# Eight inner tiles begun early and finished among whole ones, own buffers for the accumulated block, norms in single steps, squares on VectorE

## The chip, the cores and the metric

The kernel runs on one core of one Trainium2 chip. The metric is the device time of one execution, in microseconds (us); less is better. TensorE does the matmuls, VectorE (DVE) and ScalarE (ACT) the element-wise work, GpSimd (POOL) some element-wise work and the issue of transfers that add to their target, SyncE (SP) the issue of most other transfers.

## The reference

One layer of a decoder: 512 prompt tokens and 8 sample tokens of width 2048. The part that the change touches is the end of the first sub-layer and the first half of the second:

```python
x = x + gt1[:, None, :] * (jnp.concatenate([att, rw], axis=-1) @ w_out[l])
h2 = _modulate(_rmsnorm(x, g_norm_ffn[l]), sh2, sc2)
gate, up = jnp.split(h2 @ w_ffn_in[l], 2, axis=-1)     # 2048 -> 2 x 5632
x = x + gt2[:, None, :] * ((jax.nn.silu(gate) * up) @ w_ffn_out[l])
```

where

```python
def _rmsnorm(x, g):
    y = xf * lax.rsqrt(jnp.mean(xf * xf, axis=-1, keepdims=True) + RMS_EPS)
    return (y * g.astype(jnp.float32)).astype(x.dtype)
def _modulate(h, shift, scale):
    return h * (1.0 + scale[:, None, :]) + shift[:, None, :]
```

All is float32. Ahead of it stand the modulation vectors, a first norm, the combined input projection, sliding-window attention and an RWKV-7 mixer; behind it a final norm.

## The kernel before

Features lie on the 128 partitions, tokens along the rows. The 520 tokens are two halves of 260 columns (HB: 256 of the prompt, 4 samples); x is kept as eight tiles `x1[kp]` of two feature blocks each. Float32 precision is had from pairs: a block `t` is cut into `wh` (ScalarE's cast, L1244) and `wl = t - wh` (VectorE, L1245), and each product of 128 x 128 weights with 260 columns is three matmuls: `wh` with the high part, `wh` with the low part, `wl` with the high part of the operand. Four such products, on one loaded block of 128 x 512 weights, are 12 matmuls.

**Out projection, last quarter (`wout_half`).** It is done for half 0, then for half 1: 16 output blocks of 12 matmuls each per half, two to a PSUM tile. After each pair `accumulate_half` adds the gated result to x (VectorE: L1192 for the 256 prompt columns of each block, L1194 and L1195 for the samples), copies the sample columns and stores x (GpSimd, L1197, L1198), squares x (ScalarE, L1200), and adds the squares up in `acc` (GpSimd, L1203 and L1210). `norm` sums them over the partitions by a matmul with ones (L1215), takes the root and VectorE's reciprocal (L1218).

**Norms.** `norm_first` is half 0's norm. It runs as a generator in the background of half 1's matmuls: `pump`, called after each product, takes it one `yield` further. Its result is `B0`, the high and low parts of half 0's operand. `norm_second` is half 1's norm together with the combinations of the two halves that the inner projection needs: B22, T1, T2, T3, T4. It is a generator of 37 steps that `ffn_in` calls by hand. In a pair (`norm_pair`) VectorE multiplies, GpSimd copies the sample columns (L1237), ScalarE scales and shifts (L1239).

**Inner projection (`ffn_in`).** The 5632 pairs of gate and up are 44 inner tiles. In each, the weight rows of gate and up and the two halves of the 2048 features make 2 x 2 blocks a11, a12, a21, a22, and the two halves of tokens the other side; seven products in place of eight give the four results. Each of the seven is 2 groups (g) of 12 matmuls, so a whole tile has 168 matmuls. p1 and p2 (a11 with B11, a12 with B21) need half 0 alone; the other five need half 1's norm. So the first six tiles are *early* ones: their p1 and p2 (48 matmuls) are done while half 1's norm is made, 22 of its 37 steps among them, and their sum goes to DRAM (`pcd`). Then the loop over all 44 tiles runs: tiles 0 to 5 are *old*, take their sum back (`pc`) and do the other five products (120 matmuls); tiles 6 to 43 are whole. The other steps of the norm are taken in tile 0, three after each product.

Per group SyncE loads a11, a21, a12 (tag `sr`, six buffers together), a22 (tag `raw`, three) and s3 (tag `ar`, three). GpSimd issues an accumulating transfer that adds a block of weights to a21 (L1448) and one that adds to s3 (L1451; not in the second group of an old tile). VectorE then adds a21 into a11 (L1457) and a11 into a12 (L1464). When a tile is done, VectorE multiplies (L1412) and GpSimd stores the result `gd` (L1414). The order of the instructions on each engine, and of the issues on each queue, is set by the tile framework's scheduler from the order of the code; each engine takes its instructions in that order.

Of the kernel before, what the change touches and what calls it, by code (L numbers as in the profile page):

```python
# [14 lines left out]
P = 128  # L15
# [48 lines left out]
class Kern:  # L64
    def __init__(self, tc, I, O, upto="all"):
        self.tc, self.nc, self.I, self.O, self.upto = tc, tc.nc, I, O, upto
        self.n = 0
        self.bg = []
        self.free, self.done_at = {}, 0.0
        self.px = PacedCore(self)  # L70
        self.nada = 0
        self.sample_done = self.kv_done = self.decode_done = False
        self.cat_out, self.cat_in = set(), 0
        self.psc = None
        self.squares = [None, None]

# [72 lines left out]
    def run(self):  # L149
        tc, nc, I = self.tc, self.nc, self.I  # L150
        R = dict(side="right")
        with ExitStack() as st:
# [8 lines left out]
            self.x1d = [self.dr.tile([P, 2, 2, HB], F32, name=f"x1d{i}") for i in range(8)]  # L161
            self.pcd = [self.dr.tile([P, 2, HB], F32, name=f"pcd{i}") for i in range(6)]
            self.gd = [self.dr.tile([P, 2, HB], F32, name=f"gd{i}") for i in range(FT)]
# [1022 lines left out]
    def accumulate_half(self, o, n, ps, gt, h):  # L1186
# [12 lines left out]
        sq = self.fp.tile([P, 2, HB], F32, tag="n", bufs=self.nb, name=self.nm("sqh"))[:, 0:n]  # L1199
        nc.scalar.activation(sq, x, AF.Square)  # L1200
        if o == 0:
            acc = self.fp.tile([P, HB], F32, tag=f"acc{h}", name=self.nm("acc"))
            nc.gpsimd.tensor_tensor(acc, sq[:, 0], sq[:, 1], ALU.add)  # L1203
            self.squares[h] = [acc]
        elif n == 1:
            self.squares[h].append(sq[:, 0])
        else:
            acc = self.squares[h][0]
            for j in range(n):
                nc.gpsimd.tensor_tensor(acc, acc, sq[:, j], ALU.add)  # L1210

    def norm(self, h, ps, nc):

        for i, a in enumerate(self.squares[h]):
            nc.tensor.matmul(ps[:, 0:HB], self.ones, a, start=i == 0, stop=i == 2)  # L1215
        r = self.fp.tile([P, HB], F32, tag=f"rstd{h}", name=self.nm("rstdh"))
        nc.scalar.activation(r, ps[:, 0:HB], AF.Sqrt, bias=self.eps_r, scale=1.0 / 2048)
        nc.vector.reciprocal(r, r)  # L1218
        return r
# [11 lines left out]
    def norm_pair(self, nc, h, kp, r, us):  # L1231

        k = 2 * kp
        hb = self.fp.tile([P, 2, HB], F32, tag="n", bufs=self.nb, name=self.nm("hb"))
        nc.vector.tensor_tensor(hb[:, :, 0:256], self.x1[kp][:, :, h, 0:256],
                                r[:, 0:256].unsqueeze(1).broadcast_to([P, 2, 256]), ALU.mult)
        nc.gpsimd.tensor_copy(hb[:, :, 256:HB], us[:, k:k + 2])  # L1237
        for i in range(2):
            nc.scalar.activation(hb[:, i, 0:256], hb[:, i, 0:256], AF.Identity, bias=self.mod[:, SH2 + k + i, 0:1],  # L1239
                                 scale=self.G[:, k + i, 0:1])  # L1240
        return hb

# [4 lines left out]
    def norm_first(self, psum):  # L1247

        nc = self.px
        r = self.norm(0, psum("ssq2"), nc)  # L1250
        yield
        us = self.norm_start(nc, 0, r)
        self.hb0 = []
        for kp in range(8):
            hb = self.norm_pair(nc, 0, kp, r, us)
            self.hb0.append(hb)
            ks = slice(2 * kp, 2 * kp + 2)
            self.cut(nc, self.B0[0][:, ks], self.B0[1][:, ks], hb)
            for _ in range(4):
                self.done_at = self.now()  # L1260
                yield

    def norm_second(self, psum):
# [6 lines left out]
        for kp in range(4):  # L1270
# [7 lines left out]
            yield  # L1278
            less(b12, b22, b12)
            put(self.B22, kp, b22)  # L1280
            yield
            less(b22, b22, b11)
            put(self.T1, kp, b11)
            yield
# [84 lines left out]
    def ffn_in(self, st):  # L1369
# [15 lines left out]
        src = lambda ht, row, col, g: I["w_fi"][2 * ht + row][:, 1024 * col + 512 * g:1024 * col + 512 * g + 512]  # L1385

        def load(ht, row, col, g, tag="sr"):
            pool, n = (self.w, 3) if tag == "raw" else (sp, 6)
            t = pool.tile([P, 512], F32, tag=tag, bufs=n, name=self.nm(tag))
            nc.sync.dma_start(t, src(ht, row, col, g))  # L1390
            return t
# [42 lines left out]
        rest = iter(())  # L1434
        for ht in range(FT):
            pc = ct("pc", 3)
# [6 lines left out]
            for g in range(2):  # L1443
                a11, a21 = load(ht, 0, 0, g), load(ht, 1, 0, g)
                a22 = load(ht, 1, 1, g, "raw")
# [3 lines left out]
                if not (old and g):  # L1449
                    nc.sync.dma_start(s3, src(ht, 0, 0, g))  # L1450
                    nc.gpsimd.dma_start(s3, src(ht, 1, 0, g), accum_op=ALU.add)  # L1451
                if not old:
                    product(p12[:, 0], weights(a11), B11, g)
                    product(p12[:, 1], weights(a12), B21, g)
                    if g == 1:
                        first_sums(pc, p12)
                nc.vector.tensor_tensor(a11, a21, a11, ALU.add)  # L1457
                for ps, a, b in ((p45[:, 1], a21, T1), (p67[:, 0], a11, T2), (p67[:, 1], s3, T3),
                                 (p45[:, 0], a22, T4), (p3[:, 0], a12, B22)):
                    product(ps, weights(a), b, g)  # L1460
                    if b is T1:
# [3 lines left out]
                        next(rest, None)  # L1465
                    if ht == 0:
                        for _ in range(3):
                            next(norm, None)
                    if g == 0:
# [227 lines left out]
```

## Time and profile before

| | |
|---|---|
| three runs | 2688.58, 2691.93 (median), 2697.04 us |
| the profiled execution's own time | 2691.33 us |
| its span | 2689.6 us |
| mean granted TensorE clock | 0.973 |
| TensorE busy | 2576.4 us, 96% of the span |
| VectorE busy | 1707.8 us, 63% |
| ScalarE busy | 1109.5 us, 41% |
| GpSimd busy | 421.8 us, 16% |
| mean DMA rate | 170 GB/s |

The span is the time from the first to the last instruction of the profiled execution; 1.7 us of its own time lie outside it. The granted clock is the share of full speed that TensorE was given. Shares are means over stages of different kinds: the out projection's half 1 begins at 1183.4 us of the span, the early tiles at 1219.8, the old tiles at 1264.9, the whole ones at 1389.4, and they end at 2163.5.

### The profile page before, as it was taken

How to read it: one execution, taken by the hardware profiler on the slowest of the kernel's cores; microseconds unless marked ns; L12 is line 12 of the kernel's file. 1: busy time of each engine (PE TensorE's matmuls, PEld its weight loads, DVE VectorE, ACT ScalarE, POOL GpSimd, SP SyncE). 2: the span in 40 equal slices, each digit the busy share in tenths (PEclk: the TensorE clock that was granted, in tenths of full speed). 3: DMA queues.
4: the chain of work that ended last, by engine and by line, in shares of the span. 5: the costliest groups of instructions: out<-in, count | busy, mean ns of one | idle time of the engine just before them, and what ended most of it. 6: DMA issues, size and time to landing. Idle time of an engine off the chain costs nothing. (4 is left out here: it accounts for less than half of the span.)

```text
span 2689.6 us, 59198 instructions
## 1 busy us (share of the span) xinstructions
PE 2576.4 (96%) x23405; PEld 2366.7 (88%) x23405; DVE 1707.8 (63%) x3825; ACT 1109.5 (41%) x2136; POOL 421.8 (16%) x567
## 2 busy tenths in 40 slices
PE   6899999999999999988889999999999999999997
PEld 4577778787787899887789999999999999999997
DVE  3466676776767355678667777777777763443456
ACT  3133444455533334555334444444444432222225
POOL 1012122122112000043111221212212100000004
PEclk9899899999989999999889999999999999999999
DMA  7965454555556663246677777777777663343333
GB/s 278 324 196 167 123 153 150 159 155 162 152 159 213 206 221 107 92 149 193 181 187 198 194 194 192 196 196 191 199 195 193 165 204 93 122 127 97 120 103 108
DMA packets 241879, 458.10 MB, mean 170 GB/s; under 512 B 33936, under 2 KB 45120, under 8 KB 241568
## 3 DMA queue, kind: packets, MB, share of 16 engines
q1 hardware_dynamic: 206928, 377.78, 43.3%
q0 software_dynamic: 34032, 75.49, 13.5%
q8 instruction: 183, 3.00, 0.5%
q10 hardware_dynamic: 640, 1.05, 0.2%
q14 instruction: 96, 0.79, 0.1%
HBM read 420.15 MB, written 35.06 MB: 169 GB/s over the span
## 5 line engine op out<-in xcount | busy, mean ns | idle before, releaser
L88 ACT CAST wh<-raw 128x512 fp32r<-128x512 f32 (+2 forms) x405 | 246.3, 611 | 489.0 <-PE pf L98 286.6
L98 PE MATMUL pf<-go,wh 128*128 128x260 f32 x2560 | 414.1, 281 | 0.0
L1244 ACT CAST wh<-sr 128x512 fp32r<-128x512 f32 x416 | 258.3, 621 | 367.2 <-PE pm L1404 326.3
L91 DVE TENSOR_TENSOR wl<-raw,wh 128x512 fp32r<-128x512 f32 (+2 forms) x405 | 281.8, 697 | 172.2 <-ACT wh L88 159.2
L98 PEld LDWEIGHTS pf<-go,wh 128*128 128x128 f32 x2560 | 353.9, 188 | 0.1
L1245 DVE TENSOR_TENSOR wl<-sr,wh 128x512 fp32r<-128x512 f32 x416 | 286.8, 690 | 98.4 <-ACT wh L1244 88.8
L98 PE MATMUL pm<-hH,wh 128*128 128x260 f32 (+1 forms) x1248 | 297.5, 318 | 1.7 <-ACT hH L143 1.6
L1404 PE MATMUL pm<-xT,wh 128*128 128x260 f32 x1408 | 269.6, 291 | 1.7 <-ACT wh L1244 1.7
L98 PE MATMUL pf<-go,wl 128*128 128x260 f32 x1280 | 267.7, 282 | 0.0
L98 PE MATMUL pm<-hL,wh 128*128 128x260 f32 (+1 forms) x1248 | 265.0, 292 | 0.2 <-DVE hL L144 0.2
L98 PE MATMUL pm<-hH,wl 128*128 128x260 f32 (+1 forms) x1248 | 262.3, 290 | 0.1
L1404 PE MATMUL pm<-T,wh 128*128 128x260 f32 x1408 | 258.9, 284 | 2.4 <-ACT wh L1244 2.4
L98 PEld LDWEIGHTS pm<-hH,wh 128*128 128x128 f32 (+1 forms) x1248 | 195.5, 192 | 50.2 <-issue 32.3
L1404 PEld LDWEIGHTS pm<-xT,wh 128*128 128x128 f32 x1408 | 223.4, 194 | 7.6 <-ACT wh L1244 2.2
L1404 PEld LDWEIGHTS pm<-T,wh 128*128 128x128 f32 x1408 | 217.6, 189 | 2.8 <-ACT wh L1244 2.8
L1404 PE MATMUL pm<-xT,wl 128*128 128x260 f32 x704 | 196.8, 290 | 16.8 <-DVE wl L1245 16.8
L1404 PE MATMUL pm<-B0H,wl 128*128 128x260 f32 x704 | 199.4, 283 | 5.3 <-DVE wl L1245 5.1
L1404 PE MATMUL pm<-B0H,wh 128*128 128x260 f32 x704 | 200.2, 284 | 3.6 <-DVE acct L1194 2.7
L98 PEld LDWEIGHTS pm<-hH,wl 128*128 128x128 f32 (+1 forms) x1248 | 197.5, 192 | 6.0 <-DVE wl L91 2.1
L98 PEld LDWEIGHTS pm<-hL,wh 128*128 128x128 f32 (+1 forms) x1248 | 198.0, 192 | 5.4 <-issue 2.0
L1404 PE MATMUL pm<-T,wl 128*128 128x260 f32 x704 | 199.2, 284 | 2.0 <-DVE wl L1245 2.0
L98 PEld LDWEIGHTS pf<-go,wl 128*128 128x128 f32 x1280 | 201.0, 188 | 0.0
(417 smaller groups left out, 5196.5 us busy)
## 6 DMA issues: line engine op xcount, KB each, us to landing
sr<-in_w_fi SPq DMA_DIRECT2D x264, 256.0 KB, 3.6
ar<-in_w_ada SPq DMA_DIRECT2D x256, 256.0 KB, 3.1
raw<-in_w_fo SPq DMA_DIRECT2D x176, 256.0 KB, 2.6
raw<-in_w_in SPq DMA_DIRECT2D x148, 256.0 KB, 3.6
araw<-in_w_ada SPq DMA_DIRECT2D x64, 512.0 KB, 6.3
raw<-in_w_fi SPq DMA_DIRECT2D x112, 256.0 KB, 3.3
sr<-in_w_fi POOLq DMA_DIRECT2D x88, 256.0 KB, 4.7
s<-in_w_fi SPq DMA_DIRECT2D x82, 256.0 KB, 3.6
```

Of the source, the lines that this page charges most:

```text
L88: nc.scalar.copy(wh[:, :n], raw[:, :n])
L91: nc.vector.tensor_tensor(wl[:, :n], raw[:, :n], wh[:, :n].bitcast(F32), ALU.subtract)
L98: nc.tensor.matmul(ps[:m, bank, :HB], w, a[:, k, h, :], start=first and i == 0, stop=last and i == 2, skip_group_check=True,)
L1244: nc.scalar.copy(H, src)
L1245: nc.vector.tensor_tensor(L, src, H.bitcast(F32), ALU.subtract)
L1404: nc.tensor.matmul(ps[:, :HB], x[:, s], y, start=g == k == i == 0, stop=g == 1 and k == 3 and i == 2, skip_group_check=True)
```

## The change

1. Eight tiles are early in place of six. The old tiles are no longer the first of the loop: each stands behind four whole ones (places 4, 9, ..., 39).
2. a21 leaves the `sr` buffers. It goes by turns to four buffers of the pool `xp` that hold nothing at that time (tags sq, rstd, sq, acc); a11 and a12 keep the six of `sr`.
3. `norm_first` begins eight steps later and takes six steps for a pair, three ahead of the cut and three behind it, in place of four. `norm_second` has 45 steps with one operation (or one cut) in each; 30 of them are taken in the early tiles, 14 in the first group of the first whole tile, the last ahead of its second group. ScalarE copies the sample columns in place of GpSimd.
4. In the out projection VectorE adds the squares up, those of one accumulation when the next one is made. In the last block, after the second projection, GpSimd goes on doing it at once.

```diff
-            self.pcd = [self.dr.tile([P, 2, HB], F32, name=f"pcd{i}") for i in range(6)]
+            self.pcd = [self.dr.tile([P, 2, HB], F32, name=f"pcd{i}") for i in range(8)]
...
         nc.scalar.activation(sq, x, AF.Square)
+        if gt == GT1:
+            self.add_squares(nc.vector)
+            self.pending = h, o, n, sq
+        else:
+            self.pending = h, o, n, sq
+            self.add_squares(nc.gpsimd)
+
+    def add_squares(self, eng):
+        if not self.pending:
+            return
+        h, o, n, sq = self.pending
+        self.pending = None
         if o == 0:
             acc = self.fp.tile([P, HB], F32, tag=f"acc{h}", name=self.nm("acc"))
-            nc.gpsimd.tensor_tensor(acc, sq[:, 0], sq[:, 1], ALU.add)
+            eng.tensor_tensor(acc, sq[:, 0], sq[:, 1], ALU.add)
             self.squares[h] = [acc]
         elif n == 1:
             self.squares[h].append(sq[:, 0])
         else:
             acc = self.squares[h][0]
             for j in range(n):
-                nc.gpsimd.tensor_tensor(acc, acc, sq[:, j], ALU.add)
+                eng.tensor_tensor(acc, acc, sq[:, j], ALU.add)
 
     def norm(self, h, ps, nc):
 
+        self.add_squares(self.nc.vector)
         for i, a in enumerate(self.squares[h]):
...
-        nc.gpsimd.tensor_copy(hb[:, :, 256:HB], us[:, k:k + 2])
         for i in range(2):
             nc.scalar.activation(hb[:, i, 0:256], hb[:, i, 0:256], AF.Identity, bias=self.mod[:, SH2 + k + i, 0:1],
                                  scale=self.G[:, k + i, 0:1])
+        nc.scalar.copy(hb[:, :, 256:HB], us[:, k:k + 2])
         return hb
...
         nc = self.px
+        def rest(n):
+            for _ in range(n):
+                self.done_at = self.now()
+                yield
+
+        yield from rest(8)
         r = self.norm(0, psum("ssq2"), nc)
         yield
         us = self.norm_start(nc, 0, r)
         self.hb0 = []
         for kp in range(8):
-            hb = self.norm_pair(nc, 0, kp, r, us)
-            self.hb0.append(hb)
+            self.hb0.append(self.norm_pair(nc, 0, kp, r, us))
+            yield from rest(3)
             ks = slice(2 * kp, 2 * kp + 2)
-            self.cut(nc, self.B0[0][:, ks], self.B0[1][:, ks], hb)
-            for _ in range(4):
-                self.done_at = self.now()
-                yield
+            self.cut(nc, self.B0[0][:, ks], self.B0[1][:, ks], self.hb0[kp])
+            yield from rest(3)
...
             less(b12, b22, b12)
+            yield
             put(self.B22, kp, b22)
             yield
             less(b22, b22, b11)
+            yield
             put(self.T1, kp, b11)
...
+        places = (("sq", 2), ("rstd", 1), ("sq", 2), ("acc", 1))
+
         def load(ht, row, col, g, tag="sr"):
             pool, n = (self.w, 3) if tag == "raw" else (sp, 6)
+            if tag in places:
+                pool, (tag, n) = self.xp, tag
             t = pool.tile([P, 512], F32, tag=tag, bufs=n, name=self.nm(tag))
...
-        for ht in range(FT):
+        order = list(range(early, FT))
+        for ht in range(early):
+            order.insert(4 + 5 * ht, ht)
+        for i, ht in enumerate(order):
...
-                a11, a21 = load(ht, 0, 0, g), load(ht, 1, 0, g)
+                a11, a21 = load(ht, 0, 0, g), load(ht, 1, 0, g, places[(2 * i + g) % 4])
...
+                if i == 0 and g == 1:
+                    for _ in norm:
+                        pass
                 if not old:
-                    product(p12[:, 0], weights(a11), B11, g)
-                    product(p12[:, 1], weights(a12), B21, g)
+                    for col, a, b in ((0, a11, B11), (1, a12, B21)):
+                        product(p12[:, col], weights(a), b, g)
+                        if i == g == 0:
+                            next(norm, None)
+                            next(norm, None)
...
-                    if ht == 0:
-                        for _ in range(3):
-                            next(norm, None)
+                    if i == g == 0:
+                        next(norm, None)
+                        next(norm, None)
```

**GpSimd's queue among the old tiles.** Before, from the old tiles on; sr_... is an a21, s_... an s3, gd_130 and gd_131 the results of tiles 0 and 1:

```order
L1448 DMA sr_15861<-in_w_fi 128x512
L1451 DMA s_2222_15867<-in_w_fi 128x512
L1448 DMA sr_15957<-in_w_fi 128x512
L1414 DMA gd_130<-cu_15815 128x520
L1448 DMA sr_16063<-in_w_fi 128x512
L1451 DMA s_2257_16069<-in_w_fi 128x512
L1448 DMA sr_16159<-in_w_fi 128x512
L1414 DMA gd_131<-cu_16017 128x520
```

Now, around the first old tile, at place 4; sq_16891 and rstd_16987 are its a21 of both groups, s_2391_16897 its s3, sq_17093 and acc_17221 the a21 of the whole tile at place 5, and gd_142 and gd_143 the results of the whole tiles at places 2 and 3:

```order
L1474 DMA sq_16891<-in_w_fi 128x512
L1477 DMA s_2367_16756<-in_w_fi 128x512
L1474 DMA rstd_16987<-in_w_fi 128x512
L1477 DMA s_2391_16897<-in_w_fi 128x512
L1437 DMA gd_142<-cu_16576 128x520
L1474 DMA sq_17093<-in_w_fi 128x512
L1474 DMA acc_17221<-in_w_fi 128x512
L1477 DMA s_2427_17099<-in_w_fi 128x512
L1474 DMA sq_17362<-in_w_fi 128x512
L1437 DMA gd_143<-cu_16845 128x520
```

The accumulating transfers of the old tile have moved ahead of the result of the tile two before it, and those of the tile behind it ahead of the result of the tile before it.

**VectorE at the start of the first norm, in half 1 of the out projection.** Before; x_1591 and x_1593 are the first two tiles of x, po the PSUM tile, rstdh the reciprocal root, us the sample columns, hb the pairs:

```order
L1192 SCALAR_TENSOR_TENSOR x_1591_11653<-po_14666,mod,x_1591_11653 128x256
L49 RECIPROCAL rstdh_14680<-rstdh_14680 128x260
L1192 SCALAR_TENSOR_TENSOR x_1591_11653<-po_14666,mod,x_1591_11653 128x256
L49 TENSOR_TENSOR us_14692<-scat,rstdh_14680 128x64
L49 TENSOR_TENSOR hb_14696<-x_1591_11653,rstdh_14680 128x2x256
L49 TENSOR_TENSOR us_14692<-us_14692,Gm 128x64
L49 TENSOR_TENSOR hb_14721<-x_1593_11655,rstdh_14680 128x2x256
L49 TENSOR_TENSOR us_14692<-us_14692,mod 128x64
L1194 TENSOR_TENSOR acct_14728<-po_14666,mod 128x8
```

Now; acc_14719 is the first sum of half 1's squares, wl and raw belong to the next weights:

```order
L1192 SCALAR_TENSOR_TENSOR x_1591_11655<-po_14668,mod,x_1591_11655 128x256 x2
L1194 TENSOR_TENSOR acct_14705<-po_14668,mod 128x8
L91 TENSOR_TENSOR wl_15030<-raw_15027,wh_15029 128x512
L1195 TENSOR_TENSOR x_1591_11655<-x_1591_11655,acct_14705 128x2x4
L1258 TENSOR_TENSOR wl_15083<-raw_15080,wh_15082 128x512
L49 RECIPROCAL rstdh_14724<-rstdh_14724 128x260
L1215 TENSOR_TENSOR acc_14719<-sqh_14712 128x260
L49 TENSOR_TENSOR us_14736<-scat,rstdh_14724 128x64
L49 TENSOR_TENSOR hb_14740<-x_1591_11655,rstdh_14724 128x2x256
```

The reciprocal and what follows from it have moved behind the first accumulation of half 1, and an addition of squares has come in.

## Rows read from the trace of the kernel before

**Rows 1.** Windows: length, busy (count) PE PEld DVE ACT POOL, clock, DMA, GB/s.

```profile
1600.00:2000.00 400.00, 400.00 (x3301) 397.23 (x3300) 296.96 (x510) 187.65 (x314) 80.01 (x99) 1.00 0.74 195
```

**Rows 2.** Windows by stage: halves 0 and 1, early, old tiles 0, 4, 5, whole tiles.

```profile
1158.00:1183.40 25.40, 23.66 (x187) 22.56 (x187) 21.20 (x49) 13.75 (x23) 17.21 (x25) 1.00 0.63 209
1183.40:1219.80 36.40, 27.57 (x198) 26.64 (x198) 29.58 (x63) 22.81 (x42) 24.51 (x44) 0.91 0.33 108
1219.80:1264.90 45.10, 38.95 (x293) 36.39 (x294) 36.54 (x62) 28.09 (x55) 8.86 (x17) 1.00 0.67 208
1264.90:1289.80 24.90, 19.46 (x124) 17.75 (x123) 21.86 (x39) 12.16 (x22) 7.76 (x5) 0.86 0.63 177
...
1353.20:1374.60 21.40, 16.26 (x122) 16.05 (x121) 11.99 (x23) 6.84 (x11) 3.16 (x4) 0.84 0.61 160
1374.60:1389.40 14.80, 14.80 (x122) 14.55 (x121) 11.01 (x20) 6.86 (x11) 3.45 (x5) 1.00 0.82 231
...
1389.40:2163.50 774.10, 774.10 (x6388) 768.83 (x6387) 578.01 (x992) 365.52 (x612) 152.56 (x192) 1.00 0.74 194
```

**Rows 3.** Waits, old tiles 1 to 4: us in total, times, longest us.

```profile
DVE sr L1457 <- DMA sr<-in_w_fi: 20.4, 5, 5.8
...
PE pm L1404 <- DVE wl L1245: 17.9, 5, 5.1
```

**Rows 4.** Timeline of GpSimd, old tile 2: start, duration, instruction [idle before <-releaser].

```profile
1314.56 0.58 POOL L1414 DMA_DIRECT2D gd<-cu  x1 [8.93 <-DVE cu L1412]
...
1317.36 0.85 POOL L1448 DMA_DIRECT2D sr<-in_w_fi  x1 [2.22 <-ACT wh L1244]
```

**Rows 5.** Timeline of VectorE, the same tile.

```profile
1323.20 0.69 DVE L1457 TENSOR_TENSOR sr<-sr,sr 128x512 f32<-128x512 f32 x1 [4.23 <-DMA sr<-in_w_fi]
...
1324.54 0.68 DVE L1245 TENSOR_TENSOR wl<-s,wh 128x512 fp32r<-128x512 f32 x1
1325.14 0.68 DVE L1245 TENSOR_TENSOR wl<-raw,wh 128x512 fp32r<-128x512 f32 x1
```

**Rows 6.** Timeline of TensorE, the same tile.

```profile
1325.88 0.59 PE L1404 MATMUL pm<-xT,wl 128*128 128x260 f32 x1 [3.61 <-DVE wl L1245]
```

**Rows 7.** Line L1215: the second norm's sums, ns min/median/max, first and last start.

```profile
L1215 PE MATMUL ssq<-sqh,cst x4: 381/382/382, 1224.7 to 1225.3; 128*128 128x260 f32 x4
```

**Rows 8.** Timeline of VectorE, early stage.

```profile
1226.98 1.77 DVE L1218 RECIPROCAL rstdh<-rstdh 128x260 f32<-128x260 f32 x1
...
1230.16 0.42 DVE L1409 TENSOR_TENSOR pc<-pm,pc 128x260 f32<-128x260 f32 x1
...
1234.91 0.70 DVE L1272 TENSOR_TENSOR hb<-hb,hb 128x520 f32<-128x520 f32 x1 [2.05 <-POOL hb L1237]
```

**Rows 9.** Timeline of GpSimd, early stage.

```profile
1233.23 0.89 POOL L1448 DMA_DIRECT2D sr<-in_w_fi  x1 [5.47 <-issue]
...
1234.37 1.28 POOL L1237 COPY hb<-us 128x8 f32<-128x8 f32 x3
```

**Rows 10.** Groups by line and form, VectorE, half 1: busy us, mean ns.

```profile
L49 DVE TENSOR_TENSOR B0L<-hb,B0H 128x520 fp32r<-128x520 f32 x8 | 7.7, 966 | 0.0
...
L49 DVE TENSOR_TENSOR hb<-x,rstdh 128x512 f32<-128x512 f32 x8 | 6.7, 852 | 0.0
L1245 DVE TENSOR_TENSOR wl<-raw,wh 128x512 fp32r<-128x512 f32 x3 | 3.7, 1245 | 0.5 <-ACT wh L1244 0.5
L1195 DVE TENSOR_TENSOR x<-x,acct 128x8 f32<-128x8 f32 x7 | 2.3, 335 | 0.1
```

**Rows 11.** The same view, VectorE, half 0.

```profile
L91 DVE TENSOR_TENSOR wl<-raw,wh 128x512 fp32r<-128x512 f32 x16 | 12.0, 755 | 4.2 <-ACT wh L88 4.2
...
L1195 DVE TENSOR_TENSOR x<-x,acct 128x8 f32<-128x8 f32 x7 | 3.3, 471 | 0.0
L1184 DVE TENSOR_TENSOR x<-x,acct 128x8 f32<-128x8 f32 x1 | 0.2, 160 | 0.0
```

**Rows 12.** Timeline of TensorE, half 1.

```profile
1202.86 0.56 PE L98 MATMUL po<-cH,wh 128*128 128x260 f32 x1 [3.27 <-DVE acct L1194]
```

More of the change, by code (lines that the diff above doesn't have):

```diff
@@ L74, in __init__ @@
         self.psc = None
-        self.squares = [None, None]
+        self.squares, self.pending = [None, None], None
     def nm(self, s):
```

## The prediction

> **What bounds the kernel now.** I began with the page (TensorE 96% busy, clock 0.973 on average), then cut the stretch that the change touches into windows, one for each stage. In the steady part 400 us hold 3301 matmuls of 260 columns at granted clock 1.00 [rows 1]: 0.1212 us each. A whole inner tile has 168, so 20.36 us, and the 38 of them take 774.1 us, 20.37 each [rows 2]: the steady part is TensorE alone and can't be made shorter by waiting less. An old tile has 120, so 14.54 us. Only the last of the six runs near that (14.8 us); the first takes 24.9 and the four between, from 1289.8 to 1374.6, take 84.8 together, 21.2 each, the last of them at clock 0.84 [rows 2]. So about 6.4 us are lost in each of four tiles, 10 in the first.
>
> The view of waits over those four tiles says where [rows 3]: TensorE waits 17.9 us for VectorE's `wl`, five times, and VectorE waits 20.4 us, five times, at L1457 for a transfer into `sr`. In order of time for one tile: GpSimd's queue first waits for the product of the tile before (`gd`), then issues the accumulating transfer into a21 at 1317.36 [rows 4]; VectorE's add of that a21 into a11, which belongs to the next group, stands 4.23 us for it and starts at 1323.20; behind it, in order, stand `wl` of s3 and of a22, which TensorE needs for the present group [rows 5]; TensorE stops 3.61 us and goes on at 1325.88 [rows 6]. That is 3.6 to 5.1 us of standstill, and the rest up to 6.4 is the lower granted clock, which the window of such a tile shows as 0.84 and the steady window as 1.00. So the late thing is the transfer: a21 can be asked for only when one of six shared buffers comes free and GpSimd's queue comes by; issue to use is 5.8 us, while an old tile gives only 7.3 us per group.
>
> Ahead of that: half 1 of the out projection has 192 matmuls, 23.3 us, and takes 36.4. The early stage has 6 x 48 matmuls, 34.9 us, plus six of the second norm's sums (the last four in 0.6 us from first to last start and 0.38 for that one [rows 7]; 1.3 for six, an estimate), and takes 45.1 with VectorE busy for 36.54 [rows 2]: there VectorE's work is about as long as TensorE's.
>
> **The change, part by part.**
>
> *Two more early tiles, nothing else.* Matmuls are the same 7392. Two whole tiles leave the end (36 x 20.37 in place of 38: -40.7 us); two old tiles and two early ones come in. At the bare rate that is 2 x (14.54 + 5.82) = 40.7: the part itself is worth 0, and what counts is the loss in each stage. In the sum the -40.7 stands alone; the tiles that come in are counted in the terms of the old tiles and of the early stage.
>
> *Old tiles.* Their place (four whole tiles between) and a21's own four buffers act on the same wait. By the order, the accumulating transfers of an old tile are issued ahead of the `gd` of the tile two before it, where before they stood one group ahead and behind a `gd`; with six `sr` buffers for a11 and a12 alone, loads reach three groups ahead in place of two. Lead in time: about two whole groups of 10.2 us against 5.8 to 6 us from issue to use [rows 4, 5]; I take the wait as gone. Supply: an old tile wants 12 blocks of 256 KB besides pc and gd, 3.68 MB in 14.8 us, some 250 GB/s; the last old tile of before ran at 231 GB/s, share 0.82, without a stop [rows 2], and here four whole tiles (193 GB/s, estimate of the same kind: 3.94 MB in 20.37) stand between to run ahead in. So each old tile costs 14.8 by that row: 8 x 14.8 = 118.4 in place of 124.5, **-6.1**. Bounds: 14.54 x 8 = 116.3 below, 21.2 x 8 = 169.6 above, if nothing helps. I take the low end, as the row without an early wait lies there.
>
> *Early stage.* 32 products at 1.456 (12 matmuls) = 46.6 + 1.3 = 47.9 us for TensorE. VectorE, by the order: 32 `wl`, 8 of hb, 13 subtractions, 15 cuts of the second norm, all of 512 or 520 columns and, as two `wl` in a row, 0.60 apart [rows 5], 68 x 0.60 = 40.8; a reciprocal 1.77; three short ones for the sample columns, 0.45 (an estimate); eight sums of 260 columns, 0.42 long [rows 8], 0.33 without the overlap that the two `wl` of 0.68 have, 2.6: 45.7. Before, 36.54 busy stood against 36.2 of TensorE and 8.9 were lost. Part of that loss ends with the copy of the sample columns: GpSimd took three copies at 1234.37, behind 5.47 us of its own queue, and VectorE's subtraction stood 2.05 us for it [rows 8, 9]. On ScalarE (28.09 busy of 45.1 [rows 2]) the copies have room; I cost them at nothing, and without that cover eight of at most 1 us would come on the path. Left: two engines of nearly equal length that wait for each other now and then. I take 52 (4 lost): **+6.9** against 45.1; bounds 47.9 and 56.8 (8.9 lost as before), +2.8 and +11.7.
>
> *The rest of the norm.* 14 steps fall in the first whole tile's first group: eight operations, seven `wl` and two additions, 17 x 0.60 = 10.2 us of VectorE against 84 matmuls, 10.2. Before, 16 such operations fell in a group of 7.3 us, which is where tile 0's 24.9 came from [rows 2]; that loss is in the 124.5 already. Here **+2** (0 to 4).
>
> *Squares on VectorE, first norm in smaller steps.* In half 1 VectorE's operations beside GpSimd's are long. Against 0.69 for 512 columns where GpSimd is still, eight cuts of B0 take 0.966, eight of hb 0.852, three `wl` 1.245, and seven additions of 8 columns take 0.335, where 0.16 is the usual: 2.2 + 1.3 + 1.7 + 1.2 = 6.4 us [rows 5, 10]. In half 0 the same seven additions take 0.471, 2.2 us, and 16 `wl` 0.755, 1.0, so 3.2 [rows 11]. GpSimd is busy for 24.51 us of half 1 [rows 2]. TensorE stands for the accumulation queued behind, 3.27 us at the longest [rows 12]. Against that VectorE gets 13 additions of 260 columns at 0.33, 4.3 us in each half. Half 0 comes out about even (3.2 saved, 4.3 added, TensorE busy for 23.66 of 25.4 [rows 2], so little to gain): **+0.5**. In half 1 the additions come one accumulation late, so nothing waits for the square, and the first norm starts eight steps later, behind the accumulations which it stood in front of before; walked through with these durations in the new order, TensorE begins on the early tiles after 30.5 us in place of 36.4: -5.9. I take **-5**. Bounds: -8 (6.4 and 1.6 of the wait behind it) and +4.3 (all additions on the path, no stretch gained). VectorE, for its part, is already busy for 29.58 of the 36.4 us [rows 2]. The Trainium skill, page Perfetto Trace Analysis, section "Optimizing Scalar/DVE Operations", advises to move work off a saturated VectorE, to ScalarE or even GpSimd, and adds that between VectorE and GpSimd this might not help, as they share a port. By its first half the term would be +4.3, by the rows above it is -5.
>
> *a21's prefetch.* The order has four loads of it during attention, into idle buffers; TensorE is full of other matmuls there and the transfers have hundreds of us, so 0. The end (last four tiles, second projection) is untouched.
>
> Sum: -40.7 - 6.1 + 6.9 + 2 + 0.5 - 5 = -42.4, against the profiled execution's 2691.3 (the median of the runs is 0.6 above): 2648.9, **2649 us**, its own range 2641 to 2660.
>
> **The rivals.** Differences under 0.3%, 8 us, can hardly be told from no change.
>
> *A short wait stays.* The a21 transfer is early enough, but a22 or a12 of an old tile comes late: it draws 250 GB/s and the queue of loads is in order. For it: only one old tile of six ran clean; against: 231 GB/s at 0.82 without a stop [rows 2]. One stop of 1.5 us and the lower clock behind it, 2.6 us a tile, 8 tiles: +21, 2670.
>
> *VectorE becomes the bound.* In half 1 it is busy for 29.58 of 36.4 us already, and 36.54 of 45.1 in the early stage [rows 2]. If the additions lie on the path (+4.3 in place of -5) and the early stage keeps its 8.9 (56.8): +14, 2663. It is what the section of Perfetto Trace Analysis in the Trainium skill named above would lead one to expect.
>
> *The other side: each old tile goes on costing what it did.* VectorE still stands at the addition of a21 into a11, now L1489, because GpSimd's queue is held by `gd`, which comes after the tile's last product. Price 6.4 a tile, 8 x 6.4 = 51: 2649 + 51 = 2700, slower. It decides from 42.4 / 8 = 5.3 us a tile on for any loss, and 6.3 for one that can be told. Against it: the new order.
>
> *The change does nothing in the norms* (the gain of half 1 goes to another wait, as the early stage's operands are cut no sooner): +5, 2654, inside the forecast's own range.
>
> **Chances.** The forecast, with the last case in it, 0.72; VectorE the bound 0.10; short waits 0.12; the other side 0.04; 0.02 for more than I see, in either direction. Range 2640 to 2670, which holds the forecast's own range, VectorE's case and the nearer half of the short waits. Faster by over 0.3% (below 2684): 0.91; within 0.3%: 0.05 (short waits of 4 us a tile); slower: 0.04.
>
> **What would show it.** Right: windows of old tiles among the whole ones at 14.6 to 15 us and clock 1.00; no wait of VectorE at L1489 for a transfer; half 1 near 31 us with `wl` at 0.7; the early stage near 52; the 36 whole tiles at 20.4. Wrong: granted clock under 0.95 anywhere between the first whole tile and the end of the first projection, or TensorE waiting for `wl` there; an early stage above 57; half 1 above 36. The largest doubt is the early stage, where both engines are full and one late `wl` also lowers the clock.

## The result and the profile after

The changed kernel takes 2657.06 us (median of four runs, 2653.69 to 2661.14) against 2690.26 before (four runs): ratio 0.9875, 95% interval 0.9848 to 0.9902. It is faster by 33 us (26 to 41 by the interval); 2649 had been forecast, and the range held. The profiled execution took 2659.4 us, its span is 2657.6, the mean granted clock 0.981.

Windows of the changed kernel, in the columns of [rows 1]: half 1, the early stage, the first whole tile, then two whole tiles and the old tile behind them, and all from the second tile to the end of the inner projection:

```profile
1179.62:1210.74 31.12, 26.55 (x201) 25.39 (x199) 27.89 (x75) 22.72 (x49) 10.09 (x20) 0.95 0.38 124
1210.74:1264.55 53.81, 51.73 (x393) 49.74 (x394) 47.37 (x82) 38.31 (x82) 4.86 (x9) 0.97 0.66 220
1264.55:1284.92 20.37, 20.30 (x167) 19.95 (x166) 17.99 (x33) 11.31 (x21) 4.02 (x5) 1.00 0.69 187
1598.30:1619.66 21.36, 20.42 (x170) 20.20 (x169) 15.29 (x28) 9.46 (x16) 4.00 (x5) 1.00 0.78 192
1619.66:1641.21 21.55, 20.89 (x170) 20.34 (x169) 17.40 (x31) 9.60 (x16) 2.83 (x4) 1.00 0.57 159
1641.21:1655.80 14.59, 14.59 (x122) 14.46 (x121) 9.56 (x18) 6.81 (x11) 3.43 (x5) 1.00 0.99 273
1284.92:2130.53 845.61, 834.06 (x6843) 824.34 (x6841) 627.65 (x1090) 391.75 (x652) 161.24 (x205) 1.00 0.75 195
```

The old tile runs at its bare rate (14.59 us; all eight lie between 14.57 and 14.59), faster than any of [rows 2], and the clock is 1.00 from the first whole tile to the end of the inner projection. But the two whole tiles ahead of it take 21.36 and 21.55 us in place of 20.37. Over the eight old tiles the first of these two loses 6.0 us in all, the second 10.1: 16.1 us that the forecast didn't have. The old tile stands for no load (the DMA share of 0.99 is then for the tiles behind it); the stop has moved ahead of it. The waits from the second tile to the end of the inner projection name it (us in total, times, longest):

```profile
DVE s L1495 <- DMA raw<-in_w_fi: 12.0, 7, 2.1
...
DVE sr L1489 <- DMA sr<-in_w_fi: 7.9, 14, 1.8
...
PE pm L1427 <- DVE wl L1258: 5.8, 14, 0.9
PE pm L1427 <- DVE pc L1504: 5.3, 6, 1.7
```

L1489 is the addition of a21 into a11 of any tile, L1495 the subtraction a11 less a22 of an old one; all 21 waits stand in the two whole tiles ahead of an old one. So two of the prediction's own signs went against it though the time lies in its range: VectorE does wait at L1489 for a transfer, and TensorE does wait for `wl` there. VectorE's timeline over the two whole tiles (the old one starts only at 1641.21) shows them:

```profile
1615.11 0.69 DVE L1489 TENSOR_TENSOR sr<-sq,sr 128x512 f32<-128x512 f32 x1 [1.01 <-DMA sr<-in_w_fi]
1615.71 0.42 DVE L1504 TENSOR_TENSOR pc<-pm,pc 128x260 f32<-128x260 f32 x1
...
1631.13 0.69 DVE L1495 TENSOR_TENSOR s<-sr,raw 128x512 f32<-128x512 f32 x1 [1.54 <-DMA raw<-in_w_fi]
1631.74 0.68 DVE L1258 TENSOR_TENSOR wl<-sr,wh 128x512 fp32r<-128x512 f32 x1
```

and TensorE's shows who pays for them, one product later:

```profile
1616.19 0.52 PE L1427 MATMUL pm<-xT,wh 128*128 128x260 f32 x2 [0.94 <-DVE pc L1504]
...
1632.48 0.39 PE L1427 MATMUL pm<-B0H,wl 128*128 128x260 f32 x1 [0.49 <-DVE wl L1258]
```

The addition at 1615.11 is the old tile's and is wanted some 27 us later. VectorE takes its queue in order, stands for the old tile's a11 (1.01 us), and TensorE stands for what is queued behind, the `pc` of the present tile. It is the pattern of [rows 5, 6] with shorter waits.

### The profile page after: what moved, and what is told of

Read it like the earlier page. It is cut to its first block, busy times and chain, and to the rows that moved or that the text cites. A ratio compares the mean times of both kernels' runs of the same rounds, so it can differ in the third digit from the quotient of the medians.

```text
span 2657.6 us, 59190 instructions
## 1 busy us (share of the span) xinstructions
PE 2563.3 (96%) x23405; PEld 2352.7 (89%) x23405; DVE 1702.5 (64%) x3853; ACT 1109.6 (42%) x2152; POOL 387.2 (15%) x525
## 5 line engine op out<-in xcount | busy, mean ns | idle before, releaser
L1257 ACT CAST wh<-sr 128x512 fp32r<-128x512 f32 x320 | 197.9, 621 | 262.4 <-PE pm L1427 230.8
L1258 DVE TENSOR_TENSOR wl<-sr,wh 128x512 fp32r<-128x512 f32 x320 | 220.6, 690 | 83.0 <-ACT wh L1257 76.0
L1427 PE MATMUL pm<-xT,wh 128*128 128x260 f32 x1408 | 263.2, 286 | 5.5 <-DVE pc L1504 5.3
L1427 PEld LDWEIGHTS pm<-xT,wh 128*128 128x128 f32 x1408 | 217.0, 188 | 12.0 <-DVE pc L1504 7.2
L1427 PE MATMUL pm<-B0L,wh 128*128 128x260 f32 x704 | 199.5, 283 | 0.0
```

The source lines that it names most:

```text
L1257: nc.scalar.copy(H, src)
L1258: nc.vector.tensor_tensor(L, src, H.bitcast(F32), ALU.subtract)
L1427: nc.tensor.matmul(ps[:, :HB], x[:, s], y, start=g == k == i == 0, stop=g == 1 and k == 3 and i == 2, skip_group_check=True)
```

## The experiments

Two spans of one and the same kernel (the changed one, profiled twice) differ by 12.3 us, 2657.6 and 2669.9, and 9.9 of that lies ahead of half 0 of the out projection. So the table gives stages of the profiled execution beside the medians: half 1, the inner projection (early tiles included), and all from the start of half 0 to the end of the span. Starts are counted back by matmul records, good to about 1 us; the changed kernel's two profiles differ by 2.4 in the last column, and the kernel before was profiled once. Ratios are to the kernel before, run on the same chip each time; its medians there are 2690.26 us for the first comparison, 2688.23 for runs 1, 2, 7 and 9, 2691.10 for 3 to 6, and 2690.16 for 8, 10, 11 and the changed kernel again. The four kernels whose half 1 is that of before (before, 1, 2 and 3) spread from 34.1 to 39.1 us in it, the ten with the later and slower first norm from 30.1 to 31.2.

| kernel | median us | ratio, 95% interval | half 1 | inner projection | half 0 to end |
|---|---|---|---|---|---|
| before | 2690.26 | | 36.65 | 943.5 | 1532.6 |
| changed | 2657.06 | 0.9848 to 0.9902 | 31.1 | 919.8 | 1504.5 |
| changed, again | 2660.02 | 0.9872 to 0.9915 | 31.0 | 921.2 | 1506.9 |
| 1 before + buffers | 2668.60 | 0.9912 to 0.9955 | 34.1 | 922.4 | 1511.6 |
| 2 before + places | 2707.55 | 1.0056 to 1.0108 | 39.1 | 960.9 | 1553.1 |
| 3 before + holding | 2670.25 | 0.9898 to 0.9949 | 36.5 | 925.2 | 1514.6 |
| 4 before + first norm | 2687.74 | 0.9971 to 1.0010 | 30.7 | 944.9 | 1528.6 |
| 5 changed, in a row | 2671.27 | 0.9898 to 0.9963 | 31.2 | 930.3 | 1515.6 |
| 6 changed, six early | 2662.15 | 0.9865 to 0.9924 | 30.8 | 921.4 | 1507.4 |
| 7 changed, GpSimd's squares | 2660.43 | 0.9870 to 0.9920 | 30.2 | 920.6 | 1505.0 |
| 8 changed, second norm as before | 2665.13 | 0.9884 to 0.9918 | 30.8 | 924.6 | 1508.8 |
| 9 changed + holding | 2655.42 | 0.9859 to 0.9910 | 30.5 | 913.8 | 1498.3 |
| 10 changed + earlier holding | 2654.87 | 0.9839 to 0.9879 | 30.8 | 908.5 | 1490.9 |
| 11 as 10, GpSimd's squares | 2650.61 | 0.9834 to 0.9873 | 30.1 | 910.7 | 1494.5 |

**1. The buffers alone.** The kernel before with

```diff
+        places = (("sq", 2), ("rstd", 1), ("sq", 2), ("acc", 1))
...
-                a11, a21 = load(ht, 0, 0, g), load(ht, 1, 0, g)
+                a11, a21 = load(ht, 0, 0, g), load(ht, 1, 0, g, places[(2 * ht + g) % 4])
```

> The kernel before with one part of the change: a21 in its four own buffers; six early tiles, finished first and in a row, norms and squares as before. Before, the six old tiles took 124.5 us, 88 of them at the bare rate. Theory of the late transfer: the buffer was what kept a21 from being asked for, so old tiles 1 to 4 go from 21.2 to under 17 us each and tile 0 keeps its norm (about 22): old tiles together near 103 us, the time 15 to 25 us under before. Rival, supply: five old tiles in a row want 250 GB/s and nothing can run ahead, so the wait moves to other blocks (a22, a12), the tiles stay above 19 us and the gain is under 12 us. Rival, place alone: no change, 124 us.

The median is 19.6 us under that of before on the same chip. The window of the six old tiles, and two waits in it:

```profile
1272.10:1377.41 105.31, 95.65 (x723) 91.16 (x721) 80.38 (x144) 47.01 (x78) 21.77 (x27) 0.97 0.83 218
...
DVE sr L1461 <- DMA sr<-in_w_fi: 6.5, 6, 1.4
DVE s L1467 <- DMA raw<-in_w_fi: 5.0, 4, 2.2
```

105.3 us, where 103 had been expected and 124.4 were before: the buffers do work alone, though not fully. Behind the first old tile, which has the norm, the other five lose 10.8 us against their bare rate, where they lost 26.9 before.

**2. The places alone.** The kernel before with

```diff
-        for ht in range(FT):
+        order = list(range(early, FT))
+        for ht in range(early):
+            order.insert(4 + 5 * ht, ht)
+        for i, ht in enumerate(order):
...
-                    if ht == 0:
+                    if i == 0:
```

> The kernel before with another part: the six old tiles each among four whole ones, a21 still in the six shared buffers, norms and squares as before (what is left of the second norm falls in the first whole tile). Theory that both parts act on one wait: an old tile between whole ones finds a21 asked for in time only in part, 16 to 18 us each with the whole tile ahead of it, a gain of 15 to 25 us. Rival, place alone does it: old tiles at 14.6 us and no loss in the whole ones around them, a gain near 33 us. Rival, buffers alone do it: each old tile or the tile ahead of it still loses 6 us, a gain under 5 us.

Neither theory had this: 19 us slower than before. An old tile takes 20.2 to 21.9 us, the whole tile ahead of it 21.6 to 22.3 in place of 20.37, and the first whole tile, with the rest of the norm, 24.7. The fourth old tile and the whole one ahead of it:

```profile
1643.76:1665.48 21.72, 20.63 (x170) 20.28 (x169) 14.48 (x25) 9.56 (x16) 2.29 (x3) 1.00 0.58 153
1665.48:1685.87 20.39, 16.36 (x123) 16.02 (x121) 12.92 (x24) 6.84 (x11) 3.40 (x5) 0.92 0.71 179
```

The timelines of VectorE, SyncE, GpSimd, VectorE again and TensorE there, one row of each:

```profile
1658.64 0.69 DVE L1245 TENSOR_TENSOR wl<-sr,wh 128x512 fp32r<-128x512 f32 x1
...
1658.15 1.53 SPq L1390 DMA_DIRECT2D sr<-in_w_fi  x2
...
1663.42 0.87 POOL L1451 DMA_DIRECT2D sr<-in_w_fi  x1 [10.85 <-DMA sr<-in_w_fi]
...
1667.80 0.69 DVE L1460 TENSOR_TENSOR sr<-sr,sr 128x512 f32<-128x512 f32 x1 [3.99 <-DMA sr<-in_w_fi]
...
1670.15 0.59 PE L1404 MATMUL pm<-T,wl 128*128 128x260 f32 x1 [4.03 <-DVE wl L1245]
```

The load of a21 stands in SyncE's queue for a shared buffer (its second issue goes out as the `wl` of 1658.64 ends), GpSimd's accumulation for that load, VectorE's addition for the accumulation, TensorE for the `wl` behind the addition. The old tile has begun at 1665.48, and this addition is for its second group: it stands ahead of operations of the first, as before the change. The addition for the first group stands likewise in the whole tile ahead, where a21 is asked for no sooner; it costs that tile 1.4 us here.

**3. VectorE's order alone.** The kernel before, no new buffer, with VectorE's operations on an old tile's blocks held behind operations of the group ahead (`held[0]` is `cu`'s first operation of the tile ahead, `held[1]` the last cut of weights of group 0, `held[2]` the second cut of weights of the group):

```diff
-                nc.vector.tensor_tensor(a11, a21, a11, ALU.add)
+                if old and held[g]:
+                    with tc.issue_after(held[g].ins):
+                        nc.vector.tensor_tensor(a11, a21, a11, ALU.add)
...
+                    if old and g and b is T3:
+                        with tc.issue_after(held[2].ins):
+                            nc.vector.tensor_tensor(s3, a11, a22, ALU.subtract)
                     product(ps, weights(a), b, g)
```

> The kernel before with nothing but VectorE's operations on an old tile's blocks held behind the group ahead (the same holding as tried on the changed kernel). Theory of the late transfer: a21 arrives too late for its own group too (5.8 us from issue to use, and the issue waits for a shared buffer), so the old tiles stay above 19 us and the gain is under 8 us. Rival, order: VectorE stood there only because the addition was put ahead of two `wl` of the present group; then the old tiles fall to 15 to 17 us and the gain is 20 to 30 us with no buffer at all.

The rival holds. The old tiles together, and VectorE's wait at the addition (20.4 us before, [rows 3]):

```profile
1258.11:1365.12 107.01, 96.03 (x723) 90.64 (x721) 83.05 (x147) 46.44 (x78) 23.79 (x26) 0.97 0.77 209
...
DVE sr L1460 <- DMA sr<-in_w_fi: 0.3, 1, 0.3
```

107.0 us with the shared buffers of before, nearly as good as the buffers gave; behind the first the other five old tiles lose 10.6 us in place of 26.9. The scheduler also moved some 25 of SyncE's 1397 transfers among the old tiles, so VectorE's order is not quite alone; the buffers are those of before.

**4. The first norm's steps alone** (`norm_first` of the change in the kernel before).

> The kernel before with the first norm's later start and six steps a pair alone; squares on GpSimd, one accumulating buffer set, six old tiles in a row as before. Theory from the run with GpSimd's squares in the changed kernel (half 1 there 30.2 us, against 31.1 with VectorE's): the whole gain of half 1 is this step, so half 1 takes 30 to 32 us in place of 36.6 and the early stage stays near 45. Rival, the prediction's own working (VectorE freed from GpSimd's additions): half 1 stays above 34 us.

Half 1 takes 30.7 us, but the next stage 49.6 in place of 45.2:

```profile
1179.78:1210.51 30.73, 25.44 (x198) 24.38 (x199) 28.67 (x62) 21.88 (x41) 24.83 (x42) 1.00 0.39 126
1210.51:1260.10 49.59, 41.73 (x294) 39.38 (x295) 39.41 (x68) 30.87 (x61) 10.24 (x20) 0.93 0.62 193
```

The whole gain of half 1 is this step (its later start and its smaller steps together; they were not tried apart), and three quarters of it are given back in the early stage; the interval of the time holds no change.

**5. The changed kernel with its old tiles in a row** (`for i, ht in enumerate(range(FT))`).

> The changed kernel with the eight old tiles first and in a row, as the six of before; everything else of the change stays (own buffers, eight early, norms, squares). Theory now, after the first four runs: the buffers gave nearly all of the gain in the tiles, the place next to nothing, since alone it made the kernel 19 us slower. Then the inner projection takes 916 to 925 us here (919.8 in the changed kernel) and the time is within 4 us of it. Rival, the step as predicted: old tiles in a row can't run ahead of their loads (250 GB/s wanted), so with eight of them each loses 3 to 4 us, 25 to 30 in all against 16, and the time is 8 to 14 us above the changed kernel.

The rival holds in its size: 930.3 us in the inner projection, 11 to 14 us slower by the medians and 9 to 11 by the last column. Once the buffers are there, the places are worth some 10 us. The eight old tiles, and VectorE's waits in them:

```profile
1277.26:1416.15 138.89, 124.26 (x963) 119.67 (x961) 98.50 (x178) 57.93 (x96) 26.12 (x33) 0.98 0.81 217
...
DVE s L1492 <- DMA raw<-in_w_fi: 12.1, 6, 4.2
...
DVE sr L1486 <- DMA sr<-in_w_fi: 8.7, 9, 1.7
```

They lose 22.6 us against their bare rate, 2.8 each, where the whole tiles of the changed kernel lose 16.1, and the early stage takes 58.2 us, 4.7 more than in the changed kernel. VectorE stands at the same two operations as there; whether the loads are too late for the old tiles themselves, as the rival has it, or only for the places of these operations, this run doesn't show.

**6. Six early tiles in place of eight** (`range(6)` for `pcd`).

> The changed kernel with six early tiles in place of eight, each still among four whole ones. By the prediction the number of early tiles is worth nothing by itself. By the trace of the changed kernel each old tile costs 2.0 us in the two whole tiles ahead of it, so six of them lose 12 in place of 16, and the early stage has 2 x 5.82 us of matmuls less to cover the same norm: if VectorE sets its length (31 operations less 8 `wl`), it loses 4 to 8 us more. Together within 4 us of the changed kernel. Rival, the two more are a gain in the early stage that shows: 5 to 10 us slower than the changed kernel.

1507.4 us from half 0 on, against 1504.5 and 1506.9: no difference that can be told. Both parts of the expectation are there and nearly cancel: early stage and first whole tile, 69.3 us, lose 6.8 us more beyond their matmuls, and the tiles ahead of the old ones lose 11.0 in place of 16.1.

**7. Squares on GpSimd in the changed kernel.**

```diff
-        if gt == GT1:
-            self.add_squares(nc.vector)
-            self.pending = h, o, n, sq
-        else:
-            self.pending = h, o, n, sq
-            self.add_squares(nc.gpsimd)
+        self.pending = h, o, n, sq
+        self.add_squares(nc.gpsimd)
```

> The changed kernel with the squares of the out projection added by GpSimd at once, as before; the later and slower first norm stays. In the changed kernel half 1 takes from about 1183 to 1210.7 us of the span, 9 us less than before. Theory of the prediction: most of that comes from VectorE no longer running beside GpSimd's additions, so half 1 is 4 to 8 us longer here and VectorE's cuts of B0 are back near 0.9 us. Rival, norm's place: the gain comes from the first norm starting eight steps later, half 1 stays within 2 us, and TensorE's stops there stay short.

Half 1 is 1 us shorter than with VectorE's additions. The groups of VectorE in half 1 (busy us, mean ns), first with the squares on VectorE, the changed kernel:

```profile
L49 DVE TENSOR_TENSOR B0L<-hb,B0H 128x520 fp32r<-128x520 f32 x8 | 5.6, 696 | 0.0
L1222 DVE TENSOR_TENSOR acc<-acc,sqh 128x260 f32<-128x260 f32 x13 | 5.5, 425 | 0.1
L49 DVE TENSOR_TENSOR hb<-x,rstdh 128x512 f32<-128x512 f32 x8 | 5.3, 688 | 0.0
...
L1195 DVE TENSOR_TENSOR x<-x,acct 128x8 f32<-128x8 f32 x7 | 1.1, 164 | 0.0
```

then with them on GpSimd:

```profile
L49 DVE TENSOR_TENSOR hb<-x,rstdh 128x512 f32<-128x512 f32 x8 | 6.7, 860 | 0.0
L49 DVE TENSOR_TENSOR B0L<-hb,B0H 128x520 fp32r<-128x520 f32 x7 | 6.6, 949 | 0.2 <-ACT B0H L49 0.2
L1195 DVE TENSOR_TENSOR x<-x,acct 128x8 f32<-128x8 f32 x7 | 2.8, 396 | 0.0
```

The long rows do become short, as forecast. The additions then take about as much as that gave: the 13 of L1222 take 5.5 us, where the prediction had 4.3. VectorE is busy for 27.89 us of half 1 with them, 27.71 without, and one of the eight cuts of B0 (0.9 us) lies outside the second window: equal within 1 us.

**8. The second norm's steps and GpSimd's copy as before, in the changed kernel** (two `yield` taken out, `nc.scalar.copy` back to `nc.gpsimd.tensor_copy`).

> The changed kernel with norm_second's steps as before (37, some with two operations) and GpSimd's copy of the sample columns; norm_first, squares, buffers and places stay. Theory: the single steps and ScalarE's copy are what keeps the early stage from losing 9 us and more: early stage and first whole tile together 4 to 8 us longer than the changed kernel's 74.2. Rival: the eight early tiles alone give the room, within 2 us.

Early stage and first whole tile, taken together:

```profile
1213.29:1291.74 78.45, 73.30 (x558) 70.28 (x559) 66.03 (x113) 48.84 (x92) 12.66 (x22) 0.97 0.64 197
```

78.45 us against 74.2 and 74.65 in the changed kernel's two profiles: about 4 us, the low end of what was expected. But other kernels with the new steps and eight old tiles among whole ones (7, 9, 10 and 11) take 74.3 to 76.7 there, so kernels differ by 2 us for other reasons too, and 78.45 is 1.8 above the longest of them. The single steps and ScalarE's copy were not tried apart.

**9. The changed kernel with the holding of 3.**

> The changed kernel, with VectorE's three operations on blocks of an old tile (a21 into a11 in both groups, a11 less a22 in the second) held behind operations of the tile or group ahead, where the scheduler had put them up to a tile and a half earlier; nothing else. In the changed kernel the two whole tiles ahead of each old one lose 16.1 us in all, each time with VectorE standing at one of these operations for a load. Theory, order: the loads come in time for the old tile itself, so these 16 us go, old tiles stay at 14.6, whole ones are at 20.37: 2643 us against 2659 profiled. Rival, supply: the blocks are late for the old tile too, the loss moves into it (16 to 17 us each) and the time stays within 4 us.

An old tile and the whole one behind it:

```profile
1637.83:1652.99 15.16, 15.08 (x122) 14.60 (x121) 12.27 (x22) 6.85 (x11) 3.61 (x5) 1.00 0.73 198
1652.99:1674.67 21.68, 20.90 (x170) 20.34 (x169) 15.07 (x27) 9.37 (x16) 5.25 (x7) 1.00 0.94 236
```

Partly each. The whole tiles ahead are at 20.37 us, so order it was; but the old tile takes 15.17 in place of 14.58, and the tile behind it up to 1.3 more. 16.1 us become 7.7, the early stage takes 2 us more, and the median stays within 2 us of the changed kernel's.

**10. The holding, with a11 less a22 one product earlier** (`s3` behind the first cut of weights of its group, not the second); the changed kernel ran beside it again.

> The changed kernel once more, unchanged, beside the three that follow: 2657 us within the spread of its own runs (2654 to 2661); the inner projection at 918 to 922 us with some 16 us lost in the whole tiles ahead of the old ones.

> The changed kernel with VectorE's operations for an old tile held as in the first holding, but a11 less a22 right behind the first cut of weights of its group, where the first holding put it behind the second and the old tile took 15.17 us in place of 14.58. Order theory: old tiles at 14.6 us, the tiles around them at 20.37, so 16 us less in the inner projection than in the changed kernel, 904 us, and a time of 2641 to 2648. Rival: a22 is late there, the stop comes back inside the old tile, and the inner projection stays at 912 us or more.

Windows of the two whole tiles ahead of an old tile, and of that tile:

```profile
1605.54:1625.90 20.36, 20.36 (x170) 20.22 (x169) 15.15 (x27) 9.60 (x16) 3.96 (x5) 1.00 0.77 198
1625.90:1646.27 20.37, 20.37 (x170) 20.23 (x169) 15.28 (x28) 9.60 (x16) 2.29 (x3) 1.00 0.65 170
1646.27:1661.44 15.17, 15.10 (x123) 14.60 (x121) 12.18 (x22) 6.87 (x11) 3.13 (x4) 1.00 0.76 227
```

All whole tiles behind the first are clean, each old one still takes 15.17: the inner projection takes 11 to 13 us less than in the changed kernel (908.5 against 919.8 and 921.2). The old tile's last 0.6 us are no wait for a load: VectorE works from 1644.5 to 1650.1 us without a pause, and TensorE comes late to two `wl`. The time, 2654.87, is above the 2641 to 2648 expected, and only 5 us under the changed kernel's beside it. Half 0 of the profiled execution begins at 1164 us of the span, and that start varies from 1151 to 1168 among the profiles of this study; why the medians keep so little of the gain is not shown.

**11. The same with GpSimd's squares.**

> The same, with the squares of the out projection on GpSimd at once as before. Theory from the run with GpSimd's squares: the engine of these additions is worth 1 us or nothing, so within 3 us of the one without; half 1 between 30 and 31 us. Rival, the prediction's term: half 1 is 4 to 6 us longer.

30.1 us for half 1, 0.7 less than in 10, as 7 is 0.8 to 0.9 under the changed kernel. The inner projection is 2.2 longer and the last column 3.6, the median 4.3 lower, 1 more than expected: no difference that can be told. With 10 it has the lowest times of the study; on this chip the changed kernel stood at 2660.02, and its interval (0.9872 to 0.9915) barely touches theirs.

## Why the prediction came out as it did

The direction and the range were right; the change was forecast at 42 us and is 33. Of these, 26 to 28 lie in the stages that the change touches (last column of the table). By the prediction's own terms, in the profiled executions:

- **Whole tiles, -40.7.** This is the term that was mis-sized: the tiles ahead of the old ones lose 16.1 us. The rival of the short wait had the size nearly right (2.6 us a tile, 2.0 measured) and a22 as one cause, but inside the old tile and with a lower clock, which did not come (1.00 throughout). The prediction looked at what an old tile waits for and not at where VectorE's queue places its operations; runs 9 and 10 show that this place is the cause, since holding the operations makes these tiles clean (20.36 and 20.37 us).
- **Old tiles, 14.8 each.** 14.58. The reason given, that "the late thing is the transfer", was half of it. Run 3 takes 17 us off with the same buffers by order alone, run 1 takes 19 off by the buffers alone. The standstill of before needed both, a transfer that was asked for late and an addition put ahead of `wl` which the present group needed; either cure alone takes off some 16 of the 27 us that the five tiles behind the first had lost. That places and buffers act on the same wait was wrong in this form: places without buffers cost 19 us (run 2), with them they gain about 10 (run 5).
- **Early stage +6.9 and norm rest +2.** 53.81 and 20.37 us, 74.2 together where 74.4 were forecast. The split was off by 2 each way, so that the sum fits is in part luck.
- **Half 1, -5.** -5.5, but for one of the two reasons alone. The walk through the new order had both in it and was right in sum; the term named the end of the long rows first, and runs 7 and 11 show that, with the additions that pay for it, to be worth nothing (half 1 is 0.7 to 0.9 us longer), while run 4 has all of it in the first norm's new steps. Of the Trainium skill's section "Optimizing Scalar/DVE Operations" (Perfetto Trace Analysis) the part that work moved between VectorE and GpSimd might not help agrees: 31.1 us on VectorE, 30.2 on GpSimd. By its other part, that relieving a saturated VectorE may make sense, the prediction had +4.3; having the additions on VectorE costs 0.7 to 0.9 (runs 7 and 11).
- **Half 0, +0.5.** +0.3. **Number of early tiles, 0.** Run 6 agrees, by two parts that cancel.
- **a21's prefetch, 0.** No cost is shown. Half 0 starts between 1151 and 1168 us of the span in the ten profiles with the own buffers, mean 1158.6, and between 1151 and 1157 in the four without, mean 1153.9. With such a spread the starts alone show nothing. The medians say more: less the change in the last column, they lie 1.0 us under before in the mean of the ten comparisons with the own buffers (single ones from 5.2 under to 6.4 above) and 1.2 under in the three without.

Sum of the measured terms: -40.7 + 16.1 - 7.8 (old tiles, 116.6 for 124.4) + 8.6 (early stage) - 5.5 + 0.3, and -3.9 ahead of half 0, +0.8 behind the inner projection: -32.1, against -32.0 between the spans (2657.6 less 2689.6). The -3.9 ahead of half 0 is within what two profiles of one kernel differ by there (9.9) and belongs to no term.

## What to carry to other kernels

When an engine that takes its queue in order stands for a transfer, ask first whether the waiting operation is wanted now: here an addition for the next group stood ahead of operations for the present one, and putting it in its place did nearly as much as four buffers (17 us against 19). A new place in the loop or a new buffer moves such a wait by what it does to each queue's order; try the parts alone, for one of them may lose alone what it gains with the other. And cost an operation that is moved to a busy engine by its own time there, beside what its leaving frees.

## What was not expected of the hardware

Beside GpSimd's additions VectorE's operations are longer, in sum by about what the additions cost on VectorE itself: half 1 keeps it busy for 27.71 us with the additions on GpSimd and 27.89 with them on VectorE, equal within 1 us. And while an old tile runs, the DMA moves 262 to 285 GB/s at a share of about 1 without TensorE standing, more than the 231 from which the forecast took its doubt.
